# RWKV-7 recurrence: one PSUM bank for both halves of a product, separate lanes for two batches' inversions and for the outputs, and a new hand-written order of steps

## The chip, the cores and the metric

The kernel runs on one core of a Trainium2 chip, as one program. The metric is the device time in microseconds (us), lower is better. Engines are called by the names of the profile: PE (matrix products), PEld (its weight loads), DVE, ACT and POOL (vector, scalar and general engines), SP (issues DMAs; ACT issues some too). Each engine executes its own instructions in program order; engines wait for one another by semaphores.

## The reference, cut to what matters

A trunk of two layers works on 512 tokens (256 of context, 256 latent). In each layer a projection feeds two mixers; the one that matters here is a bidirectional RWKV-7 recurrence with 8 heads of width 64:

```python
def rwkv7_scan(r, w, k, v, kk, a, s0, reverse):
    def step(s, inp):
        r_t, w_t, k_t, v_t, kk_t, a_t = inp
        s = (s * w_t[:, :, None, :]
             - jnp.einsum('bhvk,bhk->bhv', s, kk_t)[..., None] * (kk_t * a_t)[:, :, None, :]
             + v_t[..., None] * k_t[:, :, None, :])
        return s, jnp.einsum('bhvk,bhk->bhv', s, r_t)
    ...
    s, ys = lax.scan(step, s0, xs, reverse=reverse)
```

It runs over the context forwards and backwards, and from the two final states over the latent tokens. The outputs of both directions are added, normalised per head, joined with a bonus term and a gate (`rwkv_readout`). Beside it stands `silu_c @ ada_w[i] + ada_b[i]`, the modulation vectors of each layer, which depend on the conditioning alone and can be computed at any time before they are used. After the mixers come an output projection and a feed-forward part: dense in layer 0, eight experts in layer 1.

## The kernel before, in words

**The recurrence in chunks.** Tokens go in chunks of 64. A *batch* is one chunk in both directions over all 8 heads: 16 matrices of 64x64, kept as tiles `[128, 2, 4, 64]`, two heads stacked on the 128 partitions (`lo` is partitions 0 to 63, `hi` 64 to 127). There are eight batches a layer, four over the context and four over the latent tokens; the second four start from the state that the first four leave. Inside a chunk the recurrence is a linear system: a triangular 64x64 matrix has to be inverted for each head and direction, and then everything is matrix products.

**Steps of one batch,** each a Python generator that yields between steps:
- `rwkv_front` (L710, letter F, nine steps): decay (L718, PE) and gate, exponentials, scaled keys and queries `arl`, `bk`.
- `rwkv_pairs` (L794, P): the pairwise products (L807, PE), masked by DVE into `AX`, `AY` (L812, two instructions for each direction); one direction transposed into `Nt` (L819); four DMAs to DRAM scratch `nsc` (L820, L821, on SP); transposes of `bk` (L830), copied to `XT`, `YT` (L832, L833).
- `rwkv_invert` (I): four DMAs bring the 16x16 diagonal blocks of all 16 matrices back as one tile `Nl` with 64 partitions (L843); POOL inverts them by 15 steps of two operations (L848, L849).
- `rwkv_load` (L): POOL's result goes to DRAM scratch `tsc` (L862) and back as `Q` (L864), all on SP.
- `rwkv_mid` (L868, M, nine steps): `R` is the transposition of `Q` (L896, DVE). `v` is transposed by PE (L901) and copied to `ux`, `uy` by ACT (L906, L907). Two stages then build the 64x64 inverse from the 16x16 ones: product (L884, L885), copy `Ym` (L912, L913), product, two `copy_predicated` for each direction into `Q` or `R` (L923) and a transposition (L924), product, copy `Ym` (L929, L930), product, copies of 32x32 blocks (L940, L941). It also scales `arl` by -2 into `AX`, `AY` (L933, L935).
- `rwkv_chain` (L946, C): what truly depends on the batch before: right side `rt` and its copy `Rs` (L961 to L966), solution `u` (L970 to L974), new state `S` (L979 to L986), the state scaled for the next batch (L989, L990 on DVE, L991 on POOL), then the output `y`: products with the state and the solution (L1004, L1008) and their copy or addition (L1013 to L1017).
- `rwkv_bonus` (B) and `rwkv_post` (L1021, Z): bonus and normalisation of a finished chunk, ending in `y` (L1059).
- `ada` (L388, A): one piece of the modulation vectors: 1 MB of weights from DRAM on ACT's DMA queue, eight products (L396), a copy `arow` (L400), two products (L404) and `mods` (L406, DVE). Layer 0's recurrence carries 24 pieces, layer 1's 16.

**How the order is set.** `play` (L214) reads a string of letters, `RW_ORDER[l]`; each letter advances one lane by one step if `may` allows it, and is skipped otherwise. Lane M holds all eight `rwkv_mid`, so batch b+1's starts after batch b's has ended. `may` lets F, P and L run ahead of the chain by a few batches. A letter D is a dummy product on PE (`warm`, L1290). Since every engine works in program order, the string is the schedule.

**PSUM.** `banks(acc=1, pf=1, pa=2, pb=2, pc=2)`: eight banks of 128 x 512. A product of 16 matrices writes its lower half to one bank of `pb` and its upper half to another:

```python
        def prod(le, lo, re, ro):
            a, b = ps("pb"), ps("pb")
            ...
                    mm(a[0:C, o], le(d, c), re(d, c), start=True, stop=True)
                    mm(b[C:P, o], lo(d, c), ro(d, c), start=True, stop=True)
```

Of the kernel before, what the change touches and what calls it, by code (L numbers as in the profile page):

```python
# [16 lines left out]
P = 128  # L17
# [9 lines left out]
NARL = 4  # L27
NH = 3
# [23 lines left out]
    ("FFFDFFDFDFDFFDFPFFPPDDPPDDFDFDFDPPFFFPIDIFPIPPPFFPFPDFDDDFFIDDFFLDMMFMPPMMPDIDMFMIFMMIDMPPFMILMB"  # L52
     "CCFFPBMCCMMMMCPFMIFFCCCMMBBCPFMAAMPPIFMMCAAAAICPAFCILPMACMPMPACMIFAMFAAACFMAMCAIMIFIFACACLFMAFAA"
     "MPAPFMFAMCMCMAFAMPPCPCMMACAAAMCFAMACMFPPIFMIFICAMAFCFAPMZPFZFMFPCPILZCCFZACMPMMPFCMAAPACCFAFFMII"
     "CACIAMFZFZZPIFPMAAFPAAMAMMLPAPAFPMAMAAPMCBFCMIBCAAFMCMAIMAACMACMAICAMFAACIFAAAMAACPMAAMPAAAMCPAL"
     "AAPAPCCPACAAMMAAPMAAAICAAAAAMAAMAAICAAMAMCAAAICMAMZMMZAMIACLZCMZAAACMAMAZMZCMZAMCMAMCMACCCAMMCAZ"
     "MCZZCCZCBCBZCZZACAAZZAAZZAADAZZZAA"),
    ("FFFAFFFAFFAFFPPPFAPPAFPFFPFIIFFAIFFAPIPPAPFFPFPPAAFFLFFFMMFPMFAIIMMFPIPFAMPPMIMFAMMMMLPAFPMMMCMC"
     "IMIFCIAAACIFACCFMCAAFLFPMPMFAMFFAPMPMPMAMCPFMCMCPMFCCFFICMICFPFPMFMIAMFPMAIPPAMMAAFMCCAPCLAFPMMC"
     "MAAFIAACAMFAIMFAMAIMCCPAFIAAAFFAMFPFAAPFPAMLAMPPAMMAACCAPIMMFAMIFCFCCAMCCAPFAIPPAMMPFAMAFPMMAIAM"  # L60
     "FPBBMMFLAACCAAPMMCAIMACMIFCIMMFICCACFFACLAMMAPPMPAMPAPMMAMACAMMAAPCCAPBICIBMAIMMMCMIACMCMCMCMCCL"
     "MMMCCMCMMCCMCMCMZMMMCZCZZCCZZZCCCZZZZZZZ"),
]
# [59 lines left out]
def body(tc, nc, A):  # L123
# [26 lines left out]

# [63 lines left out]
    def play(lanes, order, may, extra={}):  # L214
# [4 lines left out]
        step = {n: 0 for n in lanes}  # L219

        def one(n):
            if done[n] == len(lanes[n]) or not may(n, done, step):
                return False
            b = done[n]
            if next(lanes[n][b], True):
                done[n], step[n] = b + 1, 0
            else:
                step[n] += 1
            return True
        for n in order:  # L230
            if n in extra:
                extra[n](step)
            else:
                one(n)
# [153 lines left out]
    def ada(l, i0, i1, tag="acc"):  # L388

        for i in range(i0, i1):  # L390
            raw = W.get()[0][0]
# [9 lines left out]
            yield  # L401
            pt = ps(tag)
            for b in range(2):
# [3 lines left out]
                             bc(V(l, "ada_b", 2 * i, 2 * i + 2), 2), ALU.add)  # L407
            if i % 4 == 3:
# [301 lines left out]
    def rwkv_front(l, b, X, tp):  # L710
# [3 lines left out]
        up, w0, wag = X["up"], X["w0"], X["wag"]  # L714
        r, k, kk, ka = X["r"], X["k"], X["kk"], X["ka"]
# [15 lines left out]
        yield
        ve.tensor_tensor(th, az.rearrange("p (d q s) -> p d q s", d=2, s=C),
                         bc(V(l, "rw_a0"), C).rearrange("p (d q) s -> p d q s", d=2), ALU.add)
        sc.activation(th, th, AF.Tanh, scale=0.5)
        yield
        E = X["E"]
        Ei = tp.tile([P, 2, 4, C], F32, tag="Ei", name=nm("Ei"))
        F = tp.tile([P, 2, 2, 4, C], F32, tag="F", name=nm("F"))
        lt = ps("pf")
        for p in range(4):  # L740
            mm(lt[:, p * P:p * P + P], sg[:, p * P:p * P + P], K("tri2"), start=True, stop=True)

# [3 lines left out]
        yield  # L746
# [32 lines left out]
    def rwkv_bonus(l, b, X, tp):  # L779
# [4 lines left out]
        pb = ps("acc")  # L784
# [4 lines left out]
        yield  # L789
        bo = X["bo"][b] = tp.tile([P, 2, 4, C], F32, tag="bo", name=nm("bo"), bufs=2)  # L790
        ve.tensor_tensor(bo, p4, cut(X["v"], b), ALU.mult)
        yield True

    def rwkv_pairs(l, b, X, tp):  # L794
# [4 lines left out]
        AX = tp.tile([P, 2, 4, 2, C], F32, tag="AX", name=nm("AX"), bufs=3)  # L799
        AY = tp.tile([P, 2, 4, 2, C], F32, tag="AY", name=nm("AY"), bufs=3)  # L800
        n = 2 if need_y else 1
        for d in range(2):
            xp, yp = ps("pa"), ps("pa")
# [5 lines left out]
            yield  # L809
# [4 lines left out]
            yield  # L814
# [8 lines left out]
        XT = tp.tile([P, 2, 4, C], F32, tag="XT", name=nm("XT"), bufs=3)  # L823
        YT = tp.tile([P, 2, 4, C], F32, tag="YT", name=nm("YT"), bufs=3)
        xp, yp = ps("pa"), ps("pa")
        for d in range(2):
# [4 lines left out]
            yield  # L831
        sc.copy(XT, xp.rearrange("p (d q s) -> p d q s", d=2, s=C))  # L832
        sc.copy(YT, yp.rearrange("p (d q s) -> p d q s", d=2, s=C))  # L833
        X["front"][b] = (AX, AY, XT, YT, arl, Pt)
        yield True

    def rwkv_invert(b, X, tp):
# [8 lines left out]
        for s in range(NB - 1):  # L846
# [3 lines left out]
            if s % 4 == 3:  # L850
                yield
# [16 lines left out]
    def rwkv_mid(l, b, X, tp):  # L868

        AX, AY, XT, YT, arl, Pt = X["front"].pop(b)  # L870
        v = X["v"]
# [25 lines left out]
        yield  # L897
# [927 lines left out]
```

## Time and profile before

| | us |
|---|---|
| median of 3 runs | 2441.17 (2438.11 to 2442.68) |
| the profiled execution, its own time | 2437.14 |
| span of the profiled execution | 2435.3 |
| layer 0's recurrence, from 284 us | 292 |
| layer 1's recurrence, from 1270 us | 264 |

The profile is one execution. A row of a timeline gives the start in us, the duration in us, engine, line, operation, and output <- inputs by tile names; square brackets give how long the engine had been idle before and what ended that idle time. In a group of lines, the numbers behind the bar are busy us and mean ns of one, then idle time before them with what ended it. PEclk is the granted clock of PE, as a share of its upper level.

### The profile page before, as it was taken

The page shows a single profiled execution, that of the slowest core. Times are in us where ns is not written, and L with a number is a line of the kernel's source. Part 1 is how long each engine was busy: PE and PEld are TensorE (multiplying, and loading weights), DVE is VectorE, ACT ScalarE, POOL GpSimd, SP SyncE. Part 2 cuts the span into 40 slices and gives each one's busy share as a digit, 9 for nine tenths or more (in the row PEclk, how much of TensorE's full clock was granted, in tenths as well). Part 3 has the DMA queues.
Part 4 walks back from the last instruction along what each step waited for, and adds up shares of the span by engine and source line. Part 5 has one row for each costly group of instructions (what it writes and reads, how often), then busy time and mean ns, then how long its engine had stood idle before and what let it go on. Part 6 is the DMA issues. An engine that isn't in the chain of part 4 may idle for free. (4 is left out here: it accounts for less than half of the span.)

```text
span 2435.3 us, 37167 instructions
## 1 busy us (share of the span) xinstructions
PE 2185.0 (90%) x14765; PEld 1729.8 (71%) x14765; DVE 1530.2 (63%) x2236; ACT 1284.0 (53%) x1893; POOL 246.7 (10%) x597
## 2 busy tenths in 40 slices
PE   6999788878699999969978887689999999999997
PEld 3777667666488888747756666568787787877875
DVE  3637565633442333265675654478998999899996
ACT  3435434434432222344454443567787777777775
POOL 2000053420100000020003532000000000000000
PEclk8989888988899999979997889789999999999998
DMA  6211314454112322212222432548998998999991
GB/s 256 83 69 53 105 27 120 139 185 139 52 62 94 102 97 85 98 66 75 86 100 63 127 111 77 208 173 332 348 357 329 344 355 338 340 353 351 357 354 76
DMA packets 110310, 431.31 MB, mean 177 GB/s; under 512 B 51584, under 2 KB 54144, under 8 KB 61744
## 3 DMA queue, kind: packets, MB, share of 16 engines
q1 hardware_dynamic: 102800, 378.06, 43.1%
q10 hardware_dynamic: 5472, 39.85, 4.8%
q0 software_dynamic: 1856, 10.95, 1.3%
q8 instruction: 118, 1.93, 0.3%
q14 instruction: 64, 0.52, 0.1%
HBM read 418.33 MB, written 10.49 MB: 176 GB/s over the span
## 5 line engine op out<-in xcount | busy, mean ns | idle before, releaser
L289 DVE TENSOR_TENSOR lo<-raw,hi 128x1024 fp32r<-128x1024 f32 (+1 forms) x668 | 798.3, 1224 | 207.8 <-ACT hi L288 193.3
L288 ACT CAST hi<-raw 128x1024 fp32r<-128x1024 f32 (+1 forms) x668 | 685.2, 1048 | 155.7 <-PE ps_acc L1530 68.0
L1530 PE MATMUL ps_acc<-hi,gh 128*128 128x512 f32 x704 | 284.9, 405 | 0.0
L1530 PE MATMUL ps_acc<-hi,gl 128*128 128x512 f32 x704 | 278.3, 395 | 0.0
L1530 PE MATMUL ps_acc<-lo,gh 128*128 128x512 f32 x704 | 277.8, 395 | 0.0
L375 PE MATMUL ps_acc<-hh,hi 128*128 128x512 f32 (+1 forms) x448 | 180.6, 403 | 13.5 <-ACT hh L503 11.7
L375 PE MATMUL ps_acc<-hl,hi 128*128 128x512 f32 (+1 forms) x448 | 171.9, 384 | 2.9 <-POOL hl L507 2.2
L375 PE MATMUL ps_acc<-hh,lo 128*128 128x512 f32 (+1 forms) x448 | 171.6, 383 | 1.5 <-DVE lo L289 1.5
L1530 PEld LDWEIGHTS ps_acc<-lo,gh 128*128 128x128 f32 x704 | 132.1, 188 | 32.3 <-DVE lo L289 0.2
L1530 PEld LDWEIGHTS ps_acc<-hi,gl 128*128 128x128 f32 x704 | 132.4, 188 | 27.2
L1530 PEld LDWEIGHTS ps_acc<-hi,gh 128*128 128x128 f32 x704 | 132.2, 188 | 27.4
L1554 PE MATMUL ps_pc<-hi,eah 128*128 128x512 f32 x352 | 139.5, 396 | 0.0
L1554 PE MATMUL ps_pc<-lo,eah 128*128 128x512 f32 x352 | 139.0, 395 | 0.0
L1554 PE MATMUL ps_pc<-hi,eal 128*128 128x512 f32 x352 | 139.0, 395 | 0.0
L375 PEld LDWEIGHTS ps_acc<-hh,hi 128*128 128x128 f32 x448 | 88.6, 198 | 37.9 <-ACT hh L503 12.6
L1344 DVE TENSOR_TENSOR s<-s,ps_pa 128x512 f32<-128x512 f32 x22 | 15.1, 688 | 139.0 <-PE ps_pa L363 139.0
L375 PEld LDWEIGHTS ps_acc<-hl,hi 128*128 128x128 f32 x448 | 88.3, 197 | 20.0 <-POOL hl L507 3.6
L375 PEld LDWEIGHTS ps_acc<-hh,lo 128*128 128x128 f32 x448 | 88.3, 197 | 18.6 <-DVE lo L289 2.8
L533 POOL TENSOR_TENSOR xn<-macc,rstd 128x256 f32<-128x256 f32 x2 | 1.8, 924 | 853.4 <-ACT rstd L461 853.4
L848 POOL TENSOR_TENSOR Tt<-Nl,Tl 64x15 f32<-64x15 f32 (+7 forms) x240 | 71.1, 296 | 145.3 <-DMA Nl<-nsc 128.3
L396 PE MATMUL ps_acc<-raw,silc 128*32 128x256 f32 x768 | 62.4, 430 | 25.6 <-DVE mods L406 11.8
L453 PE MATMUL ps_pc<-nsq,ones 128*128 128x512 f32 (+1 forms) x112 | 55.3, 617 | 30.6 <-ACT nsq L447 30.5
(410 smaller groups left out, 4481.7 us busy)
## 6 DMA issues: line engine op xcount, KB each, us to landing
raw<-moe SPq DMA_DIRECT2D x264, 1024.0 KB, 6.1
raw<-ada ACTq DMA_DIRECT2D x34, 1024.0 KB, 5.2
raw<-win SPq DMA_DIRECT2D x28, 1024.0 KB, 4.9
raw<-fgu SPq DMA_DIRECT2D x22, 1024.0 KB, 4.9
raw<-ada SPq DMA_DIRECT2D x14, 1024.0 KB, 5.1
raw<-fdn SPq DMA_DIRECT2D x16, 448.0 KB, 3.2
res<-xc POOLq DMA_DIRECT2D x2, 2048.0 KB, 12.5
Q<-tsc SPq DMA_DIRECT2D x32, 128.0 KB, 2.8
```

Source lines behind the costliest of these rows:

```text
L288: sc.copy(hi[:, :n], t[:, a * HALF:a * HALF + n])
L289: ve.tensor_tensor(lo[:, :n], t[:, a * HALF:a * HALF + n], hi[:, :n], ALU.subtract)
L375: mm(out, a[:, o], x[:, k, n0:T], start=(k == 0 and j == 0), stop=(k == KB - 1 and j == 2))
L396: mm(pt[32 * q:32 * q + 32, :256], silc[:, k, :], raw[:, k * 256:k * 256 + 256], start=(kk == 0), stop=(kk == 1), tile_position=(0, 32 * q))
L453: mm(self.pt, ones, self.todo.pop(0)[:, :self.n], start=(self.made == 0), stop=(self.made == KB - 1))
L533: e.tensor_tensor(t, m[:, k, :], r, ALU.mult)
L848: gp.tensor_tensor(tmp[:, u, j], bc(Nl[:, s, t], s + 1), bcm(Tl[:, s, j], NB - 1 - s), ALU.mult)
L1344: ve.tensor_tensor(s, s, pu, ALU.mult)
L1530: mm(pg, x[:, k, :], ww, start=(k == 0 and j == 0), stop=(k == 7 and j == 2))
L1554: mm(pd[q], x[:, i * P:i * P + P], ww, start=(c == 0 and i == 0 and j == 0), stop=(c == 10 and i == 1 and j == 2))
```

## The change

1. **Products of `rwkv_mid` in one bank.** Lower and upper half of a product go to the same bank `pm`. One copy `Ym` over 128 partitions stands for two over 64, one `copy_predicated` for each direction stands for two. `v` is transposed by ordinary f32 products with the identity, the two directions side by side in the columns of PE, into one bank instead of two. The solution `u` of the chain goes to one bank too.
2. **Lanes.** `rwkv_mid` has two lanes: M for the even batches, N for the odd ones, so that the generator of b+1 may advance while that of b is unfinished. The output `y` leaves `rwkv_chain` and becomes `rwkv_out`, lane Y, which may run later; `S` gets three buffers for it.
3. **Banks are asked for.** A step that needs a bank yields its name first (`"pm"`, `"pa2"`); `play` lets it run only if enough are free, and `back` returns them in program order. The dummy products (D) are gone. Banks are `banks(ac=1, pf=1, pa=2, pm=2, pc=2)`.
4. **The decay product** of `rwkv_front` takes 64 rows for each direction, side by side in PE's rows, instead of 128 rows half filled with zeros; `up` shrinks from 2048 to 1536 columns. `Ei` shares its buffer with `sg`.
5. **New order strings** for both layers. In them the four steps of an inversion and the load mostly stand together (`IIIIL`).

```diff
 RW_ORDER = [
-    ("FFFDFFDFDFDFFDFPFFPPDDPPDDFDFDFDPPFFFPIDIFPIPPPFFPFPDFDDDFFIDDFFLDMMFMPPMMPDIDMFMIFMMIDMPPFMILMB"
...
+    (
+        "FAAFAFFAFFAAAAFFAFFPFFAAAAAPFFPPFFPPPAPIIIILFAFFFPFFAAAAPFFPPFFPMMPMPAMPIIIILFMAFFFPFFMBAMMAAAMPMMPP"
+        "MCAPPPABCNNCPNNCNIIIIBACYAAACNCYAYNLANANFNFAAANFFNCCACCMMCYYYMMAAYCAAACMMAMMFFAAMAAAMMFFPPMCCPPCCPPC"
+        "YYAYPFFAAYPIIIILZBAAAAFFAZFFFFFZBNNBANCAAACNFPFFANNPNAZNNPPNNPPNCCPCZACAAAACYYAAYAAAYPIIIILAAZZZZAAZ"
+        "AFFZAFFAFAZFFFPFFZAMMMCMCPMMAAAMPPMAMPPMPMPIIIILAZMCCZZACCAAACYYYAYAFFAFAAAFANNAANCNCAAANNFFFFPFFBAP"
+        "NNPPNPPNNPNCCPIIIILABCCFFCYYYFFYBAFAAAAFFFPBABMMPMCMCPPMMPPPBAMAAAAMMAAMPIIIILAAAAMAAMCCAAACCACYYYAA"
+        "YZAANNNCZNCNNZANANNAZNNZANCAAAACAZCCZZACYYYAYZZZZZZZZ"),
+    (
+        "FAAFAFFAFFAAAAFFAFFPFFAPAPPAAAPPPAPIIIILAFFAFAAAFAFAFFFPFFAAAAPFFPPAPPPAAPIIIILFAAFMMFMFFFPFFMMAAAFF"
+        "MPMPPMPPMPMPIIIIFAMFMCAAAFFAFFNNFFNNANFFNFFAAAANANNFAANAAANANACACAAACACCAACCLPPPPCMMCCMMCMPPCMCPAAAM"
+        "PIIIILFAMFFPFFMAAMPMPPMCCPPCPAAACPIIIIFFCANNAANCNCLAAANNFFANNFAFNANFFPFFNNCAAACMMCCMMCMPCMCPPMAMMPPM"
+        "PMPIIIILAFFMCAFAAACFCACFFAACYYYFFPFFYPBABPPBAANNPPNCNCPNPIIIILANAAFFNANNFNFNFNCFFFPBCCPCPPCYYYMMYMCM"
+        "CPPMMPMBMMPIIIILBMMMCCCCCYYYYZZZNNNCZNCZNZZZNNNNNNNCCCCCYYYYZZZZZZZZ")]
...
-            mm(z[d * C:d * C + C, :], wag[:, 0, chunk(b, d)], up[:, d * 512:d * 512 + 512], start=True, stop=True)
+            h = slice(d * C, d * C + C)
+            mm(z[h, :], wag[h, 0, chunk(b, d)], up[h, 0:512], start=True, stop=True)
...
         def prod(le, lo, re, ro):
-            a, b = ps("pb"), ps("pb")
+            t = ps("pm")
...
-                    mm(a[0:C, o], le(d, c), re(d, c), start=True, stop=True)
-                    mm(b[C:P, o], lo(d, c), ro(d, c), start=True, stop=True)
...
+                    mm(t[0:C, o], le(d, c), re(d, c), start=True, stop=True)
+                    mm(t[C:P, o], lo(d, c), ro(d, c), start=True, stop=True)
...
-        vt = ps("pb"), ps("pb")
-        for d in range(2):
-            for p in range(4):
-                te.transpose(vt[d][lo, p * P:p * P + P], v[:, p, chunk(b, d)], ident)
...
+        vt = ps("pm")
+        for p in range(4):
+            for h, d in ((lo, 0), (hi, 1)):
+                mm(vt[h, p * P:p * P + P], v[:, p, chunk(b, d)], ident, start=True, stop=True)
...
-        sc.copy(Ym[0:C], a)
-        sc.copy(Ym[C:P], b_)
...
+        sc.copy(Ym, t)
...
-            for h, s in ((slice(0, C), a), (slice(C, P), b_)):
-                m = K16[h, 2 * d:2 * d + 2]
...
-                ve.copy_predicated(alternate(dst[h, d], d), m, alternate(s[:, d], d))
+            m = K16[:, 2 * d:2 * d + 2]
...
+            ve.copy_predicated(alternate(dst[:, d], d), m, alternate(t[:, d], d))
...
+                     M=[rwkv_mid(l, i, X, tp) for i in range(0, 8, 2)], N=[rwkv_mid(l, i, X, tp) for i in range(1, 8, 2)],
...
+                     Y=[rwkv_out(l, i, X, tp) for i in ys], B=[rwkv_bonus(l, i, X, tp) for i in zs],
...
+            if n == "P":
+                return (b in X["scaled"] or s > 0) and gone(b - NA) and done["I"] >= b - 1
...
-            banks(acc=1, pf=1, pa=2, pb=2, pc=2)
+            banks(ac=1, pf=1, pa=2, pm=2, pc=2)
```

In the diff a P lane has seven letters a batch: two for each direction's products and masks (the fifth letter does the second masks, `Nt` and the `nsc` DMAs), one for the transposes, one for `XT`, `YT`. The first letter of M or N does `R`.

## Rows read from the trace of the kernel before

**Rows 1.** The page's totals: busy us (share of the span) x instructions, by engine.

```profile
PE 2185.0 (90%) x14765; PEld 1729.8 (71%) x14765; DVE 1530.2 (63%) x2236; ACT 1284.0 (53%) x1893; POOL 246.7 (10%) x597
```

**Rows 2.** Busy us by engine, both recurrences; then granted clock, DMA share, GB/s.

```profile
284.00:576.00 292.00, 241.60 (x3584) 191.97 (x3584) 156.04 (x332) 124.25 (x258) 96.98 (x274) 0.87 0.37 114
1270.00:1534.00 264.00, 203.18 (x3080) 161.30 (x3080) 138.05 (x311) 111.67 (x244) 90.73 (x268) 0.84 0.32 94
```

**Rows 3.** Source line L896: what ended DVE's idle time before it (us, times).

```profile
  DMA Q<-tsc: 79.3, 15
```

**Rows 4.** DVE's timeline, layer 1: last masks of batches 0 and 1, R(0).

```profile
1293.08 0.41 DVE L812 TENSOR_TENSOR AY<-ps_pa,cst 128x256 f32<-128x256 f32 x1
...
1306.19 0.41 DVE L812 TENSOR_TENSOR AY<-ps_pa,cst 128x256 f32<-128x256 f32 x1
...
1318.88 0.71 DVE L896 STREAM_TRANSPOSE R<-Q 128x512 f32<-128x512 f32 x1 [2.04 <-DMA Q<-tsc]
```

**Rows 5.** SP's timeline over the same stretch: DMA issues.

```profile
1295.09 0.56 SPq L821 DMA_DIRECT2D nsc<-Nt  x1
1297.24 1.81 SPq L843 DMA_DIRECT2D Nl<-nsc  x4
...
1315.36 1.11 SPq L864 DMA_DIRECT2D Q<-tsc  x2
1316.56 2.00 SPq L843 DMA_DIRECT2D Nl<-nsc  x4
```

**Rows 6.** DVE's timeline: some R's of both layers, one mask between.

```profile
333.07 0.70 DVE L896 STREAM_TRANSPOSE R<-Q 128x512 f32<-128x512 f32 x1
...
380.21 0.71 DVE L896 STREAM_TRANSPOSE R<-Q 128x512 f32<-128x512 f32 x1 [6.16 <-DMA Q<-tsc]
...
407.26 0.71 DVE L896 STREAM_TRANSPOSE R<-Q 128x512 f32<-128x512 f32 x1 [7.76 <-DMA Q<-tsc]
...
409.54 0.68 DVE L812 TENSOR_TENSOR AY<-ps_pa,cst 128x512 f32<-128x512 f32 x1
...
439.88 0.71 DVE L896 STREAM_TRANSPOSE R<-Q 128x512 f32<-128x512 f32 x1 [4.23 <-DMA Q<-tsc]
...
530.53 0.71 DVE L896 STREAM_TRANSPOSE R<-Q 128x512 f32<-128x512 f32 x1 [13.04 <-DMA Q<-tsc]
...
1360.11 0.71 DVE L896 STREAM_TRANSPOSE R<-Q 128x512 f32<-128x512 f32 x1 [3.46 <-DMA Q<-tsc]
...
1498.23 0.71 DVE L896 STREAM_TRANSPOSE R<-Q 128x512 f32<-128x512 f32 x1 [7.95 <-DMA Q<-tsc]
```

**Rows 7.** Tile Nl: its DMAs, from issue to landing.

```profile
DMA to landing us min/median/max: 1.6/2.2/10.1
```

**Rows 8.** Groups of instructions by line, layer 0's recurrence (284 to 576 us).

```profile
L718 PE MATMUL ps_pf<-up,wag 128*64 128x512 f32 x32 | 10.7, 751 | 10.9 <-DMA up<-up 10.9
L901 PE MATMUL ps_pb<-cst,v 128*64 128x128 f32 x64 | 8.5, 275 | 0.0
...
L923 DVE COPY_PREDICATED Q<-k,ps_pb 64x128 f32<-64x128 uint32 x16 | 4.7, 296 | 6.5 <-PE ps_pb L885 6.2
...
L912 ACT COPY Ym<-ps_pb 64x512 f32<-64x512 f32 x8 | 4.6, 579 | 21.1 <-PE ps_pb L885 18.1 <-POOL Tt L848 1.7 <-PE ps_pb L884 1.4
...
L924 DVE STREAM_TRANSPOSE R<-Q 128x256 f32<-128x256 f32 x8 | 3.6, 445 | 0.3
```

**Rows 9.** Windows of one product each (L807, L884, L980): PE and PEld busy, clock.

```profile
300.38:301.55 1.17, 1.16 (x16) 0.97 (x16) 1.00 0.07 14
505.24:506.41 1.17, 1.14 (x16) 1.00 (x16) 1.00 0.94 325
541.80:543.00 1.20, 1.15 (x16) 1.01 (x16) 1.00 0.00 0
```

**Rows 10.** DVE's timeline: the last `y` of each layer's recurrence.

```profile
574.19 0.76 DVE L1059 SCALAR_TENSOR_TENSOR y<-ps_acc,dv 128x256 f32<-128x256 f32 x2 [2.40 <-PE ps_acc L1050]
...
1531.78 0.76 DVE L1059 SCALAR_TENSOR_TENSOR y<-ps_acc,dv 128x256 f32<-128x256 f32 x2
```

More of the change, by code (lines that the diff above doesn't have):

```diff
@@ L27 @@
 NARL = 4
+NA = 3
+NQ = 2
+NU = 2
 NH = 3
@@ L212, in interleave, with play @@
                 steps(fill, rate)
-    def play(lanes, order, may, extra={}):
+    def play(lanes, order, may):
         done = {n: 0 for n in lanes}
         step = {n: 0 for n in lanes}
+        want = {n: None for n in lanes}
         def one(n):
-            if done[n] == len(lanes[n]) or not may(n, done, step):
+            w = want[n]
+            if done[n] == len(lanes[n]) or w and free[w[:2]] < int(w[2:] or 1) or not may(n, done, step):
                 return False
             b = done[n]
-            if next(lanes[n][b], True):
-                done[n], step[n] = b + 1, 0
+            want[n] = next(lanes[n][b], True)
+            if want[n] is True:
+                done[n], step[n], want[n] = b + 1, 0, None
             else:
@@ L230, in play @@
         for n in order:
[L231 to L234, printed above, removed]
+            one(n)
         while any([one(n) for n in lanes]):
@@ new lines, in rwkv_mid @@
+        p4 = vt.rearrange("p (q e s) -> p q e s", q=4, e=2)
+        for h, d in ((lo, 0), (hi, 1)):
+            sc.copy(ux[hi, d], p4[h, :, 0, :])
+            sc.copy(uy[lo, d], p4[h, :, 1, :])
+        back("pm")
+        yield "pm"
+        t = prod(*nt, *halves(Q, R))
+        yield None
+        Ym = tp.tile([P, 2, 4, C], F32, tag="Ym", name=nm("Ym"), bufs=2)
+        sc.copy(Ym, t)
+        back("pm")
+        yield "pm"
+        t = prod(*halves(R, Q), *halves(Ym))
+        yield None
@@ L933, in rwkv_mid @@
+            yield "pm" if d == 1 else None
+        t = prod(*nt, *halves(Q, R))
+        yield None
+        Ym = tp.tile([P, 2, 4, C], F32, tag="Ym", name=nm("Ym"), bufs=2)
+        sc.copy(Ym, t)
+        back("pm")
+        yield "pm"
+        t = prod(*halves(Ym), *halves(R, Q))
         sc.mul(AX[0:C, :, :, 0, :], arl[0:C, :, :, 0, :], -2.0)
-        yield
+        yield None
         sc.mul(AY[C:P, :, :, 0, :], arl[C:P, :, :, 0, :], -2.0)
@@ L993, in rwkv_chain @@
-        if not need_y:
+            for h in (lo, hi):
+                mm(u_[h, o], Wm[d][h, d, p, :], Rs[h, d, p, :], start=True, stop=True)
+        yield None
+        sc.copy(ux[lo], tiles(u_)[lo])
+        ve.tensor_copy(uy[hi], tiles(u_)[hi])
+        back("pc")
+        if need_y:
+            X["out"][b] = AX, AY, ux, uy, arl, S
+        if b == 7:
             yield True
             return
+        yield "pc"
+        s_ = ps("pc")
+        for d, p, o in mats:
+            mm(s_[lo, o], XT[:, d, p, :], ux[:, d, p, :], start=True, stop=True)
+            mm(s_[hi, o], YT[:, d, p, :], uy[:, d, p, :], start=True, stop=True)
@@ new lines, in rwkv_chain @@
+        yield None
+        t = X["S"] = tp.tile([P, 2, 4, C], F32, tag="S", name=nm("S"), bufs=3)
+        if S is None:
+            ve.tensor_copy(t, tiles(s_))
+        else:
+            ve.tensor_tensor(t, tiles(s_), S, ALU.add)
+        back("pc")
+        nx, ny = X["ux"].pop(b + 1)
+        pd = bc(Pt, C)
+        ve.tensor_tensor(nx[lo], t[lo], pd[lo], ALU.mult)
+        ve.tensor_tensor(ny[hi], t[hi], pd[hi], ALU.mult)
+        gp.tensor_tensor(t, t, pd, ALU.mult)
+        yield True
@@ L998, in rwkv_chain, with rwkv_out, tiles @@
+    def rwkv_out(l, b, X, tp):
+        yield "pc2"
+        AX, AY, ux, uy, arl, S = X["out"].pop(b)
+        mats = [(d, p, slice((4 * d + p) * C, (4 * d + p) * C + C)) for d in range(2) for p in range(4)]
+        def tiles(t):
+            return t.rearrange("p (d q s) -> p d q s", d=2, s=C)
         a, b_ = ps("pc"), ps("pc")
-        if S is None:
-            yield
-        else:
+        if S is not None:
             for n, (d, p, o) in enumerate(mats):
@@ L1288, in mixing @@
[L1288 to L1294 removed]
             W.act = True
[L1296 removed]
+            lanes, may = recurrences(l, X, tp)
+            play(lanes, RW_ORDER[l], may)
             W.act = False
[L1298 removed]
         banks(**MAIN)
```

288 lines of the change are left out of this document (133 added, 155 removed).

## The prediction

> **What bounds the kernel now.** I read the page's totals first [rows 1], then the busy time by stretch [rows 2], then who waits for whom. PE is busy 90% of the span, so at first sight the change should aim at PE. It touches only the two RWKV stretches, though: 284 to 576 us (layer 0, 292 us) and 1270 to 1534 us (layer 1, 264 us). There PE is busy 241.6 and 203.2 us, so 50 and 61 us are idle, and the granted clock is 0.87 and 0.84, between its two levels of 1.2 and 2.4 GHz; DVE and ACT are about half busy [rows 2]. No engine is full in them. What is waited for is told by one line: the transposition `R<-Q` (L896), first step of every batch's `rwkv_mid`, runs 16 times (eight batches, two layers) and finds DVE waiting for the DMA `Q<-tsc` in 15 of them, 79.3 us in all [rows 3]. A batch waits for its 16x16 inversion to come back from POOL.
>
> The round trip is seen whole in batch 0 of layer 1. The last mask of `rwkv_pairs` ends at 1293.49; `R<-Q` starts at 1318.88, on the DMA's landing [rows 4]. That is 25.4 us: `nsc` out until 1295.65, `Nl` in from 1297.24, then POOL's 30 operations and `tsc`, `Q` from 1315.36 [rows 5]. In layer 0 the same trip took 29.7 us once the `ada` pieces were streaming: mask end 410.22 to R at 439.88 [rows 6]; an `Nl` DMA lands in 1.6 us at best and 10.1 at worst [rows 7]. I call the trip T: 25.4 to 29.7 us, and take 27.5.
>
> Now the period. SP issues in program order, and `nsc` of batch b+1 stands behind `tsc` and `Q` of batch b in most batches. So where the masks of b+1 are done in time, a period is Q's two issues 1.1, four `nsc` issues of 0.56, 1.6 until the first `Nl`, and 18.1 from there to Q [rows 5]: 23.0 us. I take 25, an estimate that adds half of what traffic added to T. The R's say the rest: layer 0, batch 2 at 380.21 and batch 7 at 530.53, five periods in 150.3 us; layer 1, 1360.11 to 1498.23, 138.1 us [rows 6]. What makes this bearable is lookahead: in both layers the masks of b+1 stand ahead of R(b) on DVE, except once (batch 4 of layer 0, mask at 409.54, 2.3 us after R(3) at 407.26) [rows 6]. In the others they are early: masks(1) of layer 1 at 1306.19, R(0) at 1318.88 [rows 4].
>
> **The change part by part.** *One bank for both halves.* Per batch two `Ym` copies of 0.58 us go from ACT, and two `copy_predicated` of 0.30 us from DVE [rows 8]; I take the merged ones at the old price, since they go over as many columns and twice the partitions. The chain inside a batch is shorter by 2 x 0.58 + 2 x 0.30 = 1.8 us, and that counts only where nothing else is late, which is behind the last R: -1.8 per layer. If the merged copies took twice as long, it is 0.
>
> *The products themselves.* One costs 1.14 us in two banks [rows 9]. The trace has no two row halves writing one bank; its nearest row is the state product (L980), whose two column halves share a bank: 1.15 us for the same count [rows 9]. I take no change; the other end is each half in its turn, about double. The Trainium skill, "PSUM — Partial Sum Buffer", section "PSUM bank collisions raise a hardware error", speaks against this edit: it quotes that "different row tiles are not able to access the same PSUM bank at the same time". It also reports clean runs of two engines in different quadrants of one bank; by the quoted rule the time would be that of the third rival below, and no run here shows which holds.
>
> *Smaller PE edits.* The decay product (L718, 10.7 us for eight batches) becomes two 64-row halves side by side: up to half of it, 5 us a layer. The eight transpositions of `v` (L901, 8.5 us a layer) become f32 products in column pairs: 0 to +8.5 us [rows 8]. Both lie in PE time that the R wait covers; without this cover they are -5 to +3 a layer. The warm-up products go too, and `ada` pieces stand at the start in their place, so I take -1 us for each layer's lead-in, from the halved first product on the cold clock.
>
> *The output lane* takes two products and two copies out of the chain; it helps only if the chain was late, and R waits say that it was not. 0.
>
> *The order* is the term that matters. I wrote out the new letters step by step. `IIII` and `L` now come at one go, so `tsc` and `Q` of batch b always go ahead of `nsc` of b+1. And M and N never overlap: each starts after the other's last copies, in both layers. What has moved most is the masks. In layer 0 the DVE order from batch 2 on is: R(2), masks(3), R(3), masks(4), R(4), masks(5), R(5), masks(6), R(6), masks(7), R(7). DVE is in order, R(b) can't start before T has passed since masks(b), and masks(b+1) is queued behind R(b). So a period is T + x, x being what lies on DVE and PE from R(b) to the end of masks(b+1). Behind the waiting R stand also PE's first product of the batch and all that follows it there. On POOL, the products `S` (L991) and `bt` that now come behind the 30 operations of an inversion wait for up to 18.1 us [rows 5]; their readers (the next chain, the bonus) lie in the same gap, which R closes later still: 0. The work placed between masks(b) and R(b) can't fill T. PE has 241.6 / 8 = 30 us of work a batch in layer 0, 25 in layer 1 [rows 2], and about half of a batch's steps stand there (for batch 6: two transpositions, one product of M, two of C, two of Y, two of F, two of the bonus, one and a half `ada` pieces): some 13 to 15 us.
>
> x in layer 0: a DVE instruction over 512 columns takes 0.68 to 0.71 us (R and mask rows; S and F steps have that shape), a predicated copy with its transposition 0.30 + 0.45 = 0.75 [rows 4, 6, 8]. Batch 3 to 4: R 0.7, bonus 0.7, `mods` 0.2, S and its two products 2.1, two F steps 1.3, two predicated pairs 1.5, four masks 2.6: 9.0; pairs(4) (1.16 us [rows 9]) waits for the F step and the second pairs for the first masks, so 11. In the same way (sum alone, then with PE's waits): 2 to 3: 11.5, 16; 4 to 5: 7, 9; 5 to 6: 10.4, 11; 6 to 7: 5.3, 7. Sum 43 to 54; with PE slow after each wait, as the granted clock is after idle time now, up to 64.
>
> Layer 0, R(2) to R(7): 5 T + x = 5 x 27.5 + 54 = 191 (low 5 x 25.4 + 43 = 170, high 5 x 29.7 + 64 = 212), against 150: +41 (+20 to +62). R(0) to R(2) is two periods of 25 against 47.1 (R(0) is at 333.07): +3 (-1 to +5). Behind R(7): 44.4 us now to the last y (575.0), with four `ada` pieces in it; layer 1 has 34.3 with none [rows 6, 10]. I take 34 for the new order: -10 (-14 to -6).
>
> Layer 1, same reading: masks(3) after R(2) (x 4), masks(4) ahead of R(3) (a period of 25), masks(5) after R(4) (x 10), masks(6) after R(5) (x 2), masks(7) after R(6) (x 4.5). R(2) to R(7): 4 x 27.5 + 20.5 + 25 = 155.5 (141 to 174) against 138.1: +17 (+3 to +36). R(0) to R(2), 41.2 now from 1318.88 to 1360.11, where `Nl` of batch 1 went right behind Q at 1316.56 [rows 5]; its `nsc` must now go between: 50, +9 (+5 to +11). Behind R(7): -2 (-5 to +1).
>
> Sum: (3 + 41 - 10) + (9 + 17 - 2) - 2 = +56; ends +6 and +107. Against the profiled execution's 2437.1 (span 2435.3 and 1.8 around it) this is 2493; the median of the runs shown is 4.0 above that execution, so **2497 us**; ends 2447 and 2548.
>
> **The rivals.** *Faster: the trip is covered.* If Q's landing were no longer what R waits for, the period would be the work and no more. Place: the DVE wait before `R<-Q`. Price: at most the 79.3 us of [rows 3], and I give half, because PE's idle time of 50 and 61 us [rows 2] would be used up by other waits: 2401. It decides as soon as the work between masks(b) and R(b) is over 25 us. For: PE work of about 205 and 175 us would allow it. Against: 13 to 15 us stand there. Chance 0.10.
>
> *No difference.* Every x at its DVE sum, T at 25.4 because PE starts no `ada` piece while it waits, and both tails at their best: the sum's low end, +6, is close to it. 2441 within 5 us. For: less traffic beside the trip. Against: needs all three. Chance 0.06.
>
> *Row halves in turn.* Each product then costs some 0.9 us more [rows 9]; two or three lie in each x and all five in each tail: about 9 x 2.3 + 2 x 4.5 = +30, so 2527. For: no row shows such a pair in one bank. Against: column halves pay nothing. Chance 0.05.
>
> *It does not do what it says.* Two batches side by side doesn't occur in the letters; this is no separate time, it is part of the forecast.
>
> **How the numbers follow.** The forecast has 0.79 and 2447 to 2548; the range is that, with the case of no difference reached at its upper edge and the faster rival left out: 2446 to 2548. Some 0.2% (5 us) is what a measurement of this kernel can tell from no change. Faster: 0.10 and a touch of the case of no difference, 0.11; same 0.05; slower 0.84.
>
> **What would show it.** Right: `R<-Q` waits for `Q<-tsc` grow from 79 to some 150 us; each mask row of b+1 lies after the R of b, and R to R is 34 to 44 us in layer 0; PE idle grows with a lower granted clock in both stretches. The `Ym` copies are half as many at 0.58 us. One product row still 1.14 us. Wrong: R to R under 28 us, or R not waiting; then the loop is shorter than I read, or something else carries the order. If the product rows double, the bank is the cause.

## The result and the profile after

| | us |
|---|---|
| median of 4 runs | 2537.48 (2533.11 to 2541.61) |
| against the kernel before, run beside it | ratio 1.0400, 95% interval 1.0374 to 1.0427 |
| span of the profiled execution (2435.3 before) | 2531.3 |
| layer 0, last `y` (574.95 before) | 639.11 |
| layer 1, from layer 0's last `y` to its own (957.6 before) | 988.9 |

The change makes the kernel 98 us slower; 56 were forecast, and the range held the time. In the profiled execution the span is 96.0 us longer: 64.2 lie in layer 0 before its last `y`, 31.3 in layer 1, and the rest of the program differs by 0.5. The last `y` of each layer now (DVE's timeline; before in [rows 10]):

```profile
638.35 0.76 DVE L1105 SCALAR_TENSOR_TENSOR y<-ps_ac,dv 128x256 f32<-128x256 f32 x2
...
1627.23 0.76 DVE L1105 SCALAR_TENSOR_TENSOR y<-ps_ac,dv 128x256 f32<-128x256 f32 x2
```

The two recurrences in the view by stretch (columns as in [rows 2]):

```profile
284.00:640.00 356.00, 257.10 (x3590) 201.12 (x3588) 152.54 (x319) 114.82 (x242) 94.03 (x274) 0.79 0.29 90
1334.00:1630.00 296.00, 220.15 (x3136) 176.12 (x3136) 135.15 (x297) 101.19 (x225) 88.13 (x268) 0.79 0.27 82
```

PE idles 98.9 and 75.9 us, 50 and 61 before [rows 2], and its granted clock fell from 0.87 and 0.84 to 0.79. More idle time and a lower clock belong together here: PE is also busy 15.5 and 17 us longer with nearly the same instructions.

DVE's timeline of layer 0, with R (now L921) of batches 2, 3, 5, 6 and 7 and the last masks (L835) of batches 3 and 6:

```profile
381.59 0.71 DVE L921 STREAM_TRANSPOSE R<-Q 128x512 f32<-128x512 f32 x1 [6.27 <-DMA Q<-tsc]
...
402.13 0.68 DVE L835 TENSOR_TENSOR AY<-ps_pa,cst 128x512 f32<-128x512 f32 x1
...
432.75 0.71 DVE L921 STREAM_TRANSPOSE R<-Q 128x512 f32<-128x512 f32 x1 [14.33 <-DMA Q<-tsc]
...
520.15 0.71 DVE L921 STREAM_TRANSPOSE R<-Q 128x512 f32<-128x512 f32 x1 [8.32 <-DMA Q<-tsc]
...
532.53 0.68 DVE L835 TENSOR_TENSOR AY<-ps_pa,cst 128x512 f32<-128x512 f32 x1
...
560.29 0.71 DVE L921 STREAM_TRANSPOSE R<-Q 128x512 f32<-128x512 f32 x1 [10.36 <-DMA Q<-tsc]
...
596.26 0.71 DVE L921 STREAM_TRANSPOSE R<-Q 128x512 f32<-128x512 f32 x1 [11.63 <-DMA Q<-tsc]
```

Each mask row lies between the two R's. Before, the masks of the same two batches lay ahead of both R's (DVE's timeline of the kernel before; R(2) and R(3) are in [rows 6], the last row here is R(5)):

```profile
372.56 0.68 DVE L812 TENSOR_TENSOR AY<-ps_pa,cst 128x512 f32<-128x512 f32 x1
...
460.08 0.68 DVE L812 TENSOR_TENSOR AY<-ps_pa,cst 128x512 f32<-128x512 f32 x1
...
470.56 0.71 DVE L896 STREAM_TRANSPOSE R<-Q 128x512 f32<-128x512 f32 x1 [4.04 <-DMA Q<-tsc]
```

From R(2) to the end of masks(3) are now 21.2 us (x), from there to R(3) 29.9 (T). That x and T add up to the period is only their definition; what is to be seen is that T stays between 25.5 and 30.1 us while x goes from 1.9 to 21.2:

| from R(b) to R(b+1) | x | T | period | before |
|---|---|---|---|---|
| layer 0, 2 to 3 | 21.2 | 29.9 | 51.2 | 27.1 |
| 3 to 4 | 15.0 | 30.1 | 45.2 | 32.6 |
| 4 to 5 | 13.1 | 29.2 | 42.2 | 30.7 |
| 5 to 6 | 13.1 | 27.1 | 40.1 | 27.8 |
| 6 to 7 | 8.3 | 27.7 | 36.0 | 32.2 |
| layer 1, 2 to 3 | 6.9 | 28.6 | 35.5 | 29.0 |
| 3 to 4 (masks ahead of R) | | | 24.8 | 25.4 |
| 4 to 5 | 14.2 | 27.9 | 42.2 | 36.4 |
| 5 to 6 | 1.9 | 25.8 | 27.7 | 21.0 |
| 6 to 7 | 4.2 | 25.5 | 29.6 | 26.4 |

In one of these periods no wait for Q is left: DVE is busy until R(4) of layer 0 starts, so from 3 to 4 the work in the gap lasts as long as the trip.

### The profile page after: what moved, and what is told of

Its sections match the earlier page's. It is cut to its first block, busy times and chain, and to the rows that moved or that the text cites. A ratio compares the mean times of both kernels' runs of the same rounds, so it can differ in the third digit from the quotient of the medians.

```text
span 2531.3 us, 37162 instructions
## 1 busy us (share of the span) xinstructions
PE 2218.2 (88%) x14845; PEld 1753.3 (69%) x14845; DVE 1521.0 (60%) x2204; ACT 1265.5 (50%) x1861; POOL 240.1 (9%) x597
## 5 line engine op out<-in xcount | busy, mean ns | idle before, releaser
L386 PEld LDWEIGHTS ps_acc<-hh,hi 128*128 128x128 f32 x448 | 88.2, 197 | 36.4 <-ACT hh L517 11.6
L386 PEld LDWEIGHTS ps_acc<-hh,lo 128*128 128x128 f32 x448 | 87.9, 196 | 18.4 <-DVE lo L300 2.8
L1400 DVE TENSOR_TENSOR s<-s,ps_pa 128x512 f32<-128x512 f32 x22 | 15.1, 688 | 139.0 <-PE ps_pa L374 139.0
L467 PE MATMUL ps_pc<-nsq,ones 128*128 128x512 f32 (+1 forms) x112 | 55.4, 620 | 30.8 <-ACT nsq L461 30.7
L374 PE MATMUL ps_acc<-fhh,hi 128*128 128x512 f32 x176 | 69.1, 393 | 10.3 <-ACT fhh L517 10.3
```

The costliest lines, as they stand in the source:

```text
L374: mm(out, w[:, o:o + P], x[:, k, n0:n1], start=(n == 0 and j == 0), stop=(n == len(ks) - 1 and j == 2))
L386: mm(out, a[:, o], x[:, k, n0:T], start=(k == 0 and j == 0), stop=(k == KB - 1 and j == 2))
L467: mm(self.pt, ones, self.todo.pop(0)[:, :self.n], start=(self.made == 0), stop=(self.made == KB - 1))
L1400: ve.tensor_tensor(s, s, pu, ALU.mult)
```

## The experiments

Two of them ask whether the order is the cause, and whether anything else is. Four ask how much a late mask, and the trip itself, are worth. Two take the bank alone. The last three look for a faster kernel.

### The new code in the old order

The changed kernel's code is kept and its order strings are replaced by ones that play the steps of the kernel before one by one (the dummy products left out; the strings are cut here):

```diff
 RW_ORDER = [
-    (
-        "FAAFAFFAFFAAAAFFAFFPFFAAAAAPFFPPFFPPPAPIIIILFAFFFPFFAAAAPFFPPFFPMMPMPAMPIIIILFMAFFFPFFMBAMMAAAMPMMPP"
...
+    ("FFFFFFFFFFFFPPFFPPPPFFFPPFFFPPIIFFPIPPPFFPFPFFFIFFLMMFFMPPPMMPIMFMIFMMIMPPFMILMBBCCCFFPBNCCNNNNC"
...
```

> The changed kernel's code (one bank, merged copies, decay in 64-row halves, v by f32 products, lanes M, N, Y, no dummy products) played in exactly the order of steps of the kernel before, step for step; only the order strings differ from the changed kernel. Theory 'the order is all': the rest is worth 0 to -12 us, 2428 to 2442 us. Rival 'the lost dummy products leave PE cold': 2450 to 2480 us. Rival 'row halves in one bank take turns': 2455 us and more.

Measured: 2442.90 us, ratio to the kernel before 1.0018 (1.0008 to 1.0029). Layer 0's stretch looks like before again:

```profile
284.00:580.00 296.00, 235.88 (x3599) 186.51 (x3599) 151.59 (x315) 114.42 (x242) 95.94 (x274) 0.85 0.35 109
```

R(2) to R(7) takes 157.2 us in layer 0 and 131.6 in layer 1, where the kernel before has 150.3 and 138.1 and the changed one 214.7 and 159.8. So the order strings carry 94 of the 98 us. Everything else together (one bank, merged copies, the lanes, the 64-row decay, no dummy products) is worth +4 us, with an interval that just leaves out no change, and not the 0 to -12 expected. The lost dummy products do not leave PE cold: the granted clock is 0.85, and 0.87 before.

### A late mask in the kernel before

The reverse: the old code, and in its strings the last masks of batch b+1 held back, for the batches for which the change does it. What depends on them follows. In the first kernel they stand behind the fourth product of batch b, in the second right behind R(b). The second line of layer 0's string, before, first and second:

```diff
-     "CCFFPBMCCMMMMCPFMIFFCCCMMBBCPFMAAMPPIFMMCAAAAICPAFCILPMACMPMPACMIFAMFAAACFMAMCAIMIFIFACACLFMAFAA"
+     "CCFFPBMCCMMMMCPFMIFFCCCMMBBCPFMAAMPPIFMMCAAAAICAFCILMACMMACMFAMFAAACFMAMCAMACACMAAAMAMPPPPIIIFIF"
```

```diff
-     "CCFFPBMCCMMMMCPFMIFFCCCMMBBCPFMAAMPPIFMMCAAAAICPAFCILPMACMPMPACMIFAMFAAACFMAMCAIMIFIFACACLFMAFAA"
+     "CCFFPBMCCMMMMCPFMIFFCCCMMBBCPFMAAMPPIFMMCAAAAICAFCILMPPACMPMPACMIFAMFAAACFMAMCAIMIFIFACACLFMAFAA"
```

> The kernel before with new order strings only: the last masks of batch b+1 wait until the fourth product of batch b's rwkv_mid is issued, for b of 2 to 6 in layer 0 and of 2, 4, 5, 6 in layer 1; two banks, lanes and dummy products as before. Theory 'masks behind R': periods of T + x with T 25 to 30 us and x 8 to 14 us, so R(2) to R(7) grows by some 40 to 65 us in layer 0 (150.3 before) and by 15 to 40 us in layer 1 (138.1): 2495 to 2545 us. Rivals (bank, clock): within 10 us of 2440.

> The kernel before with new order strings only: the last masks of batch b+1 stand directly behind R of batch b (x of 2 to 4 us), for the same batches as in before_late_masks, where they stood behind the fourth product (x of 12 to 20 us). Theory 'a period is T + x': periods of 27 to 32 us against 30.1 and 27.6 us now, so 0 to 12 us more in layer 0 and 5 to 20 us in layer 1: 2442 to 2470 us, less than a third of what before_late_masks lost. Rival 'any mask behind R costs the whole trip, wherever it stands': 2500 us and more.

Measured: 2551.94 us (ratio 1.0453, 1.0404 to 1.0501) and 2464.87 us (1.0099, 1.0079 to 1.0119). DVE's timeline around batch 3's masks in layer 0, first kernel:

```profile
379.28 0.71 DVE L896 STREAM_TRANSPOSE R<-Q 128x512 f32<-128x512 f32 x1 [7.92 <-DMA Q<-tsc]
...
395.40 0.68 DVE L812 TENSOR_TENSOR AY<-ps_pa,cst 128x512 f32<-128x512 f32 x1
...
420.53 0.71 DVE L896 STREAM_TRANSPOSE R<-Q 128x512 f32<-128x512 f32 x1 [16.78 <-DMA Q<-tsc]
```

and the second:

```profile
382.97 0.71 DVE L896 STREAM_TRANSPOSE R<-Q 128x512 f32<-128x512 f32 x1 [8.57 <-DMA Q<-tsc]
...
384.19 0.67 DVE L812 TENSOR_TENSOR AY<-ps_pa,cst 128x512 f32<-128x512 f32 x1
...
414.75 0.71 DVE L896 STREAM_TRANSPOSE R<-Q 128x512 f32<-128x512 f32 x1 [7.67 <-DMA Q<-tsc]
```

x is 16.8 us in the one and 1.9 in the other, T is 24.4 and 29.9. Over the nine late periods x sums to 138.7 and 18.0 us, T to 238.5 and 272.5; so the periods of the first are 87 us longer in all, and 87 is also what lies between the two times, 114 and 26 us above the kernel before. The first time is 7 us above what was expected, with x of 11.5 to 20.3 us and not 8 to 14. (T is not a constant: of the 121 us by which x is larger, 34 come back in a shorter T. It is shorter where less work stands beside the trip; why, no run tells.) The two doses show that it isn't the position of one instruction that costs, but what lies between R(b) and the masks of b+1: it no longer lies beside a trip. The first kernel, with the old code and two banks, alone loses more than the whole change does.

### The masks first in the changed kernel

The changed kernel, its last masks of b+1 (and their front, pairs and bonus) brought ahead of R(b), written directly in front of it. A piece of layer 0's string, its lines joined:

```diff
-CCACCMMCYYYMMAAYCAAACMMAMMFFAAMAAAMMFFPPMCCPPCCPPCYYAYPFFAAYPIIIIL
+CCACCFFFFPPPPPMMCYYYMMAAYCAAACMMAMMAAMAAAMMMCCCCPCYYAYPFFAAYPIIIIL
```

> The changed kernel with new order strings only: the last masks of batch b+1 (and what they need of its front, its pairs and the bonus) are moved ahead of R of batch b, in every batch; all else keeps its order. Theory 'masks behind R' (a period is the round trip T plus x): R(2) to R(7) falls from 214.7 us in layer 0 and 159.8 us in layer 1 to five periods of 27 to 31 and of 25 to 28 us, so some 60 to 80 and 20 to 35 us go, and the time is 2425 to 2460 us, 2445 likeliest. Rival 'row halves in one bank take turns': nothing about the order matters, 2530 to 2545 us. Rival 'what was lost is the warm clock of PE, because the dummy products are gone': the clock stays low, 2500 to 2540 us.

Measured: 2509.17 us (ratio 1.0292, 1.0251 to 1.0332). Only 28 us came back, and the time is 49 us above the upper end of what was expected. In layer 1 it went as expected: R(2) to R(7) is 137.3 us there, as good as the 138.1 of the kernel before. In layer 0 it did not: 194.8 us instead of 214.7, far from the 150.3 before. (Of the 42 us that these two stretches gain, some 9 are lost between R(0) and R(2), and 9 ahead of R(0) of layer 0, where the order was not touched.) The view of R's line (columns as in [rows 3]), DVE's timeline and PE's around R(3) say why:

```profile
  DMA Q<-tsc: 45.3, 9
```

```profile
433.04 0.69 DVE L811 TENSOR_TENSOR bo<-ps_ac,v 128x512 f32<-128x512 f32 x1 [3.94 <-PE ps_ac L808]
433.65 0.68 DVE L784 TENSOR_TENSOR bk<-F,Ei 128x512 f32<-128x512 f32 x1
434.25 0.69 DVE L786 TENSOR_TENSOR arl<-r,E 128x512 f32<-128x512 f32 x1
...
440.75 0.68 DVE L834 TENSOR_TENSOR AY<-ps_pa,cst 128x512 f32<-128x512 f32 x1
...
442.27 0.71 DVE L920 STREAM_TRANSPOSE R<-Q 128x512 f32<-128x512 f32 x1
```

```profile
429.25 3.75 PE L808 MATMUL ps_ac<-bt,rk 128*128 128x128 f32 x16 [4.79 <-DVE dv L1081]
```

The wait for Q has shrunk from 107.6 to 45.3 us, and in layer 0 R(2) to R(6) have none: Q landed 5 to 21 us ahead of them. Now R waits for the masks ahead of it, these for the front of batch 4, and that stands on DVE behind the bonus (`bo`, L811), whose product on PE (L808) itself waited 4.8 us for `dv` on DVE. From the first product of that front (417.65) to the masks' end (441.43) the chain is 24 us long; written late, at the end of the gap, it ends late. So masks ahead of R are not enough: what they need of the front has to be ready early too. In the old order masks(3) end 7 us ahead of R(2).

### The length of the trip

Eight of the fifteen elimination steps are kept, in both kernels; the other seven are left out, so the inverse is not complete:

```diff
-        for s in range(NB - 1):
+        for s in range(0, NB - 1, 2):
```

> The changed kernel with 8 of the 15 elimination steps of the inversion on POOL (every second one left out), so that POOL's part of the round trip, 10 to 12 us, is about 5 us shorter; the inverse is not the true one. Theory 'a period is T + x': T stands whole in each of the nine late periods and in most of the others, so 45 to 75 us go: 2465 to 2495 us. Rival 'the stretch is bound by its work, the round trip lies beside it': under 15 us go, 2525 to 2540.

> The kernel before with the same 8 of 15 elimination steps. Theory 'trip in the period, with lookahead': R waits 79 us in all, some 5 us for each batch, so a trip 5 us shorter takes part of it, 20 to 55 us: 2385 to 2420. If periods were bound by work: 2430 to 2440.

Measured: 2475.68 us for the changed code (62 less than the changed kernel) and 2393.28 us for the old (46 less than before; ratio 0.981, 0.9793 to 0.9828). In the old code POOL's busy time in layer 0 fell from 97.0 [rows 2] to 66.1 us, 3.9 a batch, to which come the waits between its operations. The trip stands in the period of both kernels; in the changed one the same cut is worth a third more. Not in every period: from R(3) to R(4) of layer 0 it is 45.3 us with the short inversion and 45.2 without, so there the work in the gap holds R as long as the trip did.

### The bank alone

The changed kernel with the halves of a product in two banks again, and the kernel before with the halves in one:

```diff
-            t = ps("pm")
+            t, u = ps("pm"), ps("pm")
...
-                    mm(t[C:P, o], lo(d, c), ro(d, c), start=True, stop=True)
+                    mm(u[C:P, o], lo(d, c), ro(d, c), start=True, stop=True)
```

```diff
-            a, b = ps("pb"), ps("pb")
+            t = ps("pb")
```

> The changed kernel with the two halves of each rwkv_mid product in two banks again, two Ym copies and four predicated copies for each batch and stage; the order strings and everything else stay. Theory 'masks behind R': the chain inside a batch is longer by about 1.8 us; it counts in the x of the nine late periods in part and in the two tails, so 0 to +20 us, 2538 to 2558. Rival 'row halves in one bank take turns': products get 0.9 us faster each, up to 30 us less, 2508 to 2530 us.

> The kernel before with the products of rwkv_mid in one bank, one Ym copy and one predicated copy for a direction; order and the rest as before. Theory: 0 to -6 us (the 1.8 us of a batch counts behind the last R of each layer only), 2434 to 2441 us. Rival 'row halves in one bank take turns': +10 to +40 us, 2450 to 2480.

Measured: 2546.68 us (ratio 1.0435, 1.0403 to 1.0467) and 2437.22 us (0.9993, 0.9975 to 1.0012). Two banks gain nothing (9 us above the changed kernel, with intervals that overlap), and one bank gains nothing in the old order. PE's timeline of the changed kernel shows how two 64-row halves go into one bank, and the view of one product alone (L910; the columns of [rows 9]) what they cost at the upper clock:

```profile
390.62 0.27 PE L909 MATMUL ps_pm<-Ym,R 64*64 64x64 f32 x1
390.63 0.27 PE L910 MATMUL ps_pm<-Ym,R 64*64 64x64 f32 x1
```

```profile
390.60:391.78 1.18, 1.14 (x16) 1.00 (x16) 1.00 0.48 194
```

Lower and upper half start 10 ns apart and end together, and the 16 pairs take 1.14 us, as in two banks [rows 9].

### Three attempts at a shorter trip

First, the new code in the old order with `tsc` and `Q` issued by POOL, so that SP's queue is free for the next batch. Second, in the kernel before, the `nsc` DMAs of the first direction right behind their masks, and half of the `Nl` and `tsc` DMAs on POOL. Third, the early `nsc` alone.

```diff
-            sy.dma_start(image(tsc, b, q), Tl[16 * q:16 * q + 16])
+            gp.dma_start(image(tsc, b, q), Tl[16 * q:16 * q + 16])
```

```diff
+            if d == 0:
+                for e, a in enumerate((AX, AY)):
+                    h = slice(e * C, e * C + C)
+                    sy.dma_start(nsc[b % 2, :, e * 512:e * 512 + 256].rearrange("p (a s) -> p a s", s=C), a[h, 0, :, 0, :])
...
-            sy.dma_start(Nl[16 * q:16 * q + 16], image(nsc, b, q))
+            (sy, gp)[q % 2].dma_start(Nl[16 * q:16 * q + 16], image(nsc, b, q))
```

> The changed kernel's code in the old order of steps, and the six DMAs that bring the inverse back (tsc, Q) issued by POOL instead of SP, so that on SP the nsc and Nl DMAs of batch b+1 no longer stand behind those of batch b. Theory: the queueing on SP is part of the period in most batches; periods go from 25 to 30 us towards the work of a batch, 2390 to 2430 us. Rival: POOL's issuing and its wait for the tsc landing stand in its own way, so the trip grows as much, 2435 to 2470.

> The kernel before with a shorter way of the round trip and the true inverse: the nsc DMAs of the first direction are issued right behind that direction's masks, and of the four Nl and four tsc DMAs two each are issued by POOL, beside the two on SP. By the issue rows (0.45 to 0.6 us each) the trip is 2 to 3 us shorter; in before_short_inv 5 us a trip gave 46 us, so theory 'the trip stands in the period' gives 15 to 30 us less: 2410 to 2425. Rival 'POOL's queue loses by issuing what SP wins', as with all six DMAs on POOL: 2432 to 2445.

> The kernel before with one edit of before_short_trip alone: the two nsc DMAs of the first direction are issued right behind that direction's masks, all DMAs stay on SP. By the issue rows two of four issues (0.6 us each) leave the way from the last mask to the last nsc issue, about 0.7 to 1.2 us a trip; with 46 us for 5 us a trip (before_short_inv) that is 5 to 10 us less: 2429 to 2435. Rival 'the SP queue waits elsewhere, behind Q': within 3 us of before.

Measured: 2436.13 (ratio 0.9988, 0.9972 to 1.0003), 2443.34 (1.0023, 1.0005 to 1.0040) and 2442.16 us (1.0024, 1.0011 to 1.0038). None is faster; in each the rival was right. In the first POOL waits 26.6 us for `tsc` to land before it may issue `Q`. In the second POOL's half of `Nl` stands behind other work of POOL, here `bt`, so it is issued 4.8 us after SP's half (POOL's timeline, then SP's):

```profile
309.86 3.39 POOL L776 TENSOR_TENSOR bt<-F,r 128x512 f32<-128x512 f32 x1 [12.46 <-DVE F L752]
313.20 1.18 POOL L846 DMA_DIRECT2D Nl<-nsc  x2
```

```profile
308.39 0.83 SPq L846 DMA_DIRECT2D Nl<-nsc  x2
```

In the third SP still stands behind the batch before. Batch 5's masks (DVE) end at 441.5, but SP issues its last `nsc` only when `tsc` and `Q` of batch 4 are through (DVE's timeline, then SP's):

```profile
440.86 0.68 DVE L812 TENSOR_TENSOR AY<-ps_pa,cst 128x512 f32<-128x512 f32 x1
```

```profile
442.24 1.78 SPq L865 DMA_DIRECT2D tsc<-Tl  x4
445.43 1.13 SPq L867 DMA_DIRECT2D Q<-tsc  x2
449.82 1.11 SPq L824 DMA_DIRECT2D nsc<-Nt  x2
```

So a batch whose `nsc` waits behind `Q` gains nothing from an earlier issue. What can be gained was shown by the shorter inversion only.

## Why the prediction was right, point by point

| term | forecast | ends | measured |
|---|---|---|---|
| both lead-ins | -2 | | -4.0 and -0.6 |
| layer 0, R(0) to R(2) | +3 | -1 to +5 | +5.4 |
| layer 0, R(2) to R(7) | +41 | +20 to +62 | +64.4 |
| layer 0, behind R(7) | -10 | -14 to -6 | -1.6 |
| layer 1, R(0) to R(2) | +9 | +5 to +11 | +13.0 |
| layer 1, R(2) to R(7) | +17 | +3 to +36 | +21.7 |
| layer 1, behind R(7) | -2 | -5 to +1 | -2.8 |
| sum | +56 | +6 to +107 | +95.5 |

Four of the six terms that had ends lie above their upper end: R(0) to R(2) in both layers, and in layer 0 R(2) to R(7) and the tail. The sum stays inside because layer 1's widest term does, and because the range adds up all ends. That it held the time is in part luck; the direction and the place of the loss are not.

- **The mechanism was right.** The period is T + x where the masks stand behind R. Where they don't, 25 us were taken: five such periods took 24.8 to 27.9, and the four of them from R(0) to R(2), 26.2 and more, are why those two terms came out too small. The old order in the new code takes the loss away, and late masks in the old code bring it about.
- **T was nearly right:** 27.5 taken; the five in layer 0 have a mean of 28.8 and end at 30.1, just past the upper bound of 29.7 (29.9 without the one where DVE is busy up to R), the four in layer 1 27.0.
- **The term that was mis-sized is x in layer 0:** 54 taken, 64 as its upper end, 70.6 measured. The largest part of the excess lies in the first period (21.2 for 16), but all five are longer than taken. I had added up DVE's instructions and some waits for PE. PE is the fuller engine in four of the five: in the first it is busy 17.5 of 21.2 us. And part of its work there could have run in the gap: DVE's copy `uy` of chain 1 stands behind the waiting R(2), so all but the first two matrices of batch 1's output product start only after it, at the lower clock (PE's timeline; then that product alone, 30 matrices in 1.97 us at clock 0.50; the one in the gap of batch 6 takes 1.15 us for 32 at the upper):

```profile
383.08 1.97 PE L1045 MATMUL ps_pc<-arl,S 64*64 64x64 f32 x30 [5.71 <-DVE uy L1004]
```

```profile
383.05:385.10 2.05, 1.97 (x30) 1.78 (x30) 0.50 0.03 8
542.40:543.56 1.16, 1.15 (x32) 1.01 (x32) 1.00 0.00 0
```

  I named PE's first product and all that follows as queued behind the waiting R, but not a copy on DVE on which an output product hangs.
- **The gap itself** was read too low: 13 to 15 us of PE work in it. Between masks(3) and R(3) PE is busy 15.1 of 29.9 us, but in the four gaps after it 23.8, 21.2, 18.4 and 17.2 (the 18.4 is that of batch 6, the prediction's example). All stay under the 25 us from which the rival of the covered trip would have counted, and only before R(4) did the work, on DVE, last until R itself (first row: x of the first period; last row: behind R(7)):

```profile
381.59:402.81 21.22, 17.47 (x351) 14.98 (x351) 12.71 (x25) 6.81 (x16) 3.00 (x4) 0.85 0.31 105
402.81:432.75 29.94, 15.12 (x170) 11.47 (x170) 8.85 (x19) 8.23 (x19) 9.22 (x30) 0.82 0.31 91
447.79:477.91 30.12, 23.82 (x251) 16.94 (x251) 15.31 (x34) 12.55 (x24) 10.04 (x31) 0.77 0.41 125
490.97:520.15 29.18, 21.20 (x330) 17.33 (x326) 8.87 (x24) 9.68 (x21) 8.00 (x30) 0.84 0.42 130
533.21:560.29 27.08, 18.42 (x278) 16.29 (x280) 9.84 (x21) 10.30 (x24) 11.09 (x31) 0.87 0.22 62
568.55:596.26 27.71, 17.19 (x345) 13.16 (x342) 6.51 (x19) 6.63 (x16) 7.99 (x30) 0.87 0.37 106
596.26:639.11 42.85, 32.12 (x332) 24.04 (x332) 15.45 (x38) 15.62 (x24) 1.04 (x1) 0.58 0.26 94
```

- **The tail of layer 0 was wrong:** 34 taken from layer 1, 42.85 measured, outside its bounds. The granted clock is 0.58 there, with two `ada` pieces still in it; it was 0.77 in the tail before. I had not priced the clock. The long gap ahead of the tail does not explain it: in the old code with late masks DVE waits 19.8 us for R(7), and the tail still has 0.77 and 44.3 us, while the kernel with the masks first has 0.58 again with a wait of 7.0. The low clock goes with the new order of the tail; what in it, no run tells.
- **The signs.** The wait for Q was to grow from 79 to some 150 us; it grew to 107.6. DVE also works in a gap and waits there for other things, so only the last stretch of it is put down to Q; in the kernel with late masks and old code it is 142.5. R to R in layer 0 was to be 34 to 44 us; it is 36.0 to 51.2. The sum of the periods was the better sign.
- **The lead-ins** were to gain 2 us. The -4.0 of layer 0 is not shown to be a gain: with the same order up to there, R(0) starts at 329.0 us in the changed kernel, 337.2 with two banks and 337.9 with the masks first.
- **The small edits** were to be worth 0 to -5 us; in the old order all of them together are +4. The merged copies cost as before (`Ym` 0.59 us, `copy_predicated` 0.27 to 0.30) and are half as many. The decay product, up to half of which was to go, has gained nothing: its four matmuls take 1.97 us at the lower clock, 1.98 before, and 1.08 at the upper, before and now (PE's timeline):

```profile
304.43 1.97 PE L735 MATMUL ps_pf<-up,wag 64*64 64x512 f32 x4 [1.52 <-ACT Ei L769]
```

- **The rivals.** "The trip is covered" fell with the result. "No difference" needed three low ends; none came. "Row halves in turn" fell with the rows of a product. The Trainium skill, "PSUM — Partial Sum Buffer", section "PSUM bank collisions raise a hardware error", quotes that different row tiles can't access one bank at the same time. Read as one half after the other, that would have made each product about twice as long; the measured 1.14 us speaks against it for halves that write different partitions.

Two slips stand in the description ahead of the prediction: `rwkv_mid` has twelve steps, not nine, and a P lane has eight letters (two for the transposes), not seven. No term rests on them.

## What to carry to other kernels

Where a result makes a round trip over memory and another engine, look in the program order for the place where the next trip is started. If that place lies behind the instruction that waits for this trip, expect a period of the whole trip plus what lies between, as in the late periods here; if the start is to come earlier, all that it needs must come earlier too, or the wait only moves. And of the work that is meant to fill a gap, check on every engine that no step of it is queued behind the waiting instruction.

## What the runs showed of the hardware that was not expected

Two products over different 64 rows and into different partitions of one bank ran fully side by side: starts 10 ns apart, 1.14 us for 16 pairs, the same as in two banks. With half of the `Nl` DMAs issued by POOL, they landed 1.6 to 5.9 us after their issue, with a median of 2.1 (2.2 before [rows 7]); but POOL's issue stands in line behind its own arithmetic, and in the rows shown it came 4.8 us after SP's.
